# The last row of a decoder block: final product in two column halves, the norm's weight multiplied ahead of the root, the last scaling split over three store queues

## The chip, the cores and the metric

The kernel runs on one core of one Trainium2 chip. A core has a matrix engine (TensorE; PE in the profile, with its weight loads as PEld), three engines for elementwise work (VectorE, DVE; ScalarE, ACT; GpSimd, POOL), and SyncE (SP), which here only starts transfers and waits for them. Matmuls write into PSUM; the other operands lie in SBUF. Transfers can be started by SyncE, ScalarE and GpSimd, each with a queue of its own (q1, q10 and q0 in the profile), and are carried out by 16 DMA engines.

The metric is the time of one execution on the device, in microseconds.

## What is computed

One layer of a decoder block on 2048 tokens of width 1024: an adaptive norm, one wide input projection, a gated linear recurrence beside dilated window attention, a gated merge, an output projection with a gated residual, and a last RMSNorm. Only its end matters here:

```python
        merged = jax.nn.sigmoid(g_r + bg_r) * y_rnn + jax.nn.sigmoid(g_a + bg_a) * y_attn
        x = x + gate[:, None, :] * (merged @ w_o[l])
    return rms_norm(x, g_final)

def rms_norm(x, g):
    xf = x.astype(jnp.float32)
    y = xf * lax.rsqrt(jnp.mean(xf * xf, axis=-1, keepdims=True) + NORM_EPS)
    return (y * g.astype(jnp.float32)).astype(x.dtype)
```

## The kernel before

The output projection is the last stage. The 2048 rows are done in eight pairs of row blocks (`NP` = 8); a block has 128 rows, so a pair is 256 x 1024. Each pair is one level of a Strassen-like scheme with seven products of 128 x 512 (x 512) blocks instead of eight (`output_pair`, L2092). Every product is done in fp32r with the operands split into a high and a low part: `mm3` (L154) makes three matmuls for each of four slices of the inner dimension, so a product is twelve matmuls of 128 x 128 weights by 128 x 512 columns, all recorded under L152.

The products of a pair gather in the PSUM tiles X, Z, W, V and Y. VectorE and GpSimd add them to `xo`, the two blocks of x that were loaded before: `cols(p, i, j)` is column half j (512 columns) of block i of pair p. A pair's seventh product (number 6, "B22", into V) completes the right half of block 0. It is done in `last_output`; for all pairs but the last it runs inside the next pair, and the row norm follows some products later.

In the last pair nothing follows, so the order is written out by hand. `tc.manual_schedule()` keeps each engine's instructions in the order of the code. After product 5 the row block 1 is finished: `last_gain` multiplies its halves by the norm's weight `gf` on GpSimd, `square` sums squares on ScalarE (an ACTIVATE, then an ACTIVATION_READ_ACCUMULATOR that writes the sum), `mean_last` joins the two halves' sums on VectorE (L2077) and takes the root on ScalarE (L2078), and `rstd_last` (L178 to L186) makes four small operations on VectorE: a reciprocal and one correction step. `mean_first` (L2074) prepares the sum of the left half of block 0. The helper `put(j)` (L2152) scales one half of block 1 on ScalarE and stores it by SyncE's queue: `put(1)` before `last_output`, `put(0)` as its argument `between`, which runs after the root of block 0.

In `last_output` of the last pair, block 0 is finished: product 6 (L2053), the add of V to `cols(p, 0, 1)` (L2054), its square, the multiplication of `cols(p, 0, 0)` by `gf` on VectorE (L2057), the mean and the root, `put(0)`, the correction, and then the scaling with y = 1/root: ScalarE scales the left half and stores it by its own queue (L2063, L2064), and VectorE scales the right half and multiplies it by `gf` in one operation (L2065), stored by SyncE's queue (L2066). At the end of the program SyncE waits for all queues (L2227).

Of the kernel before, what the change touches and what calls it, by code (L numbers as in the profile page):

```python
# [10 lines left out]
F32 = mybir.dt.float32  # L11
F32R = mybir.dt.float32r
BF16 = mybir.dt.bfloat16
I32 = mybir.dt.int32
AF = mybir.ActivationFunctionType
ALU = mybir.AluOpType
# [4 lines left out]
P = 128  # L21
S = 2048
D = 1024
KT = D // P
NB = 4
CH = 512
H = 8
KH = KT // 2
# [62 lines left out]
def decoder_block(ctx, tc, x, c, positions, g_norm, w_mod, b_mod, w_in, b_gate, conv_w, conv_b,  # L91
                  w_a, b_a, w_x, b_x, lam, w_out_rnn, w_out_attn, w_o, g_final, cst, out):
    nc = tc.nc
    cnt = [0]

    def T(pool, shape, dt, tag, **kw):
        cnt[0] += 1
        return pool.tile(shape, dt, tag=tag, name=f"{tag}_{cnt[0]}", **kw)
# [52 lines left out]
    def mm(o, l, r, st, sp, **kw):  # L151
        nc.tensor.matmul(o, lhsT=l, rhs=r, start=st, stop=sp, **kw)  # L152

    def mm3(o, lh, ll, rh, rl, first=True, last=True, **kw):  # L154
        mm(o, lh, rh, first, False, **kw)
        mm(o, lh, rl, False, False, **kw)
        mm(o, ll, rh, False, last, **kw)
# [13 lines left out]
    def rstd_first(ss):  # L171

        nc.vector.tensor_scalar(ss[:, 0], ss[:, 0], 1.0 / D, EPS, ALU.mult, ALU.add)
        nc.scalar.activation(ss[:, 1], ss[:, 0], AF.Sqrt)

    def rstd_last(ss):
        v, y, t = (ss[:, i] for i in range(3))
        nc.vector.reciprocal(y, y)  # L178
        if y.shape[1] == 1:
            nc.vector.tensor_scalar(t, y, y, v, ALU.mult, ALU.mult)  # L180
        else:
            nc.vector.tensor_tensor(t, y, y, ALU.mult)
            nc.vector.tensor_tensor(t, t, v, ALU.mult)
        nc.vector.tensor_scalar(t, t, -0.5, 1.5, ALU.mult, ALU.add)
        if y.shape[1] == 1:
            nc.vector.tensor_scalar(y, y, t, None, ALU.mult)  # L186
        else:
            nc.vector.tensor_tensor(y, y, t, ALU.mult)
# [119 lines left out]
    first, events = {}, []  # L308
# [213 lines left out]
    B = {}  # L522
# [18 lines left out]
    outv = out[0].rearrange("(n j r) d -> n r j d", n=NB, r=4)  # L541
# [167 lines left out]
    with tc.manual_schedule():  # L709
# [87 lines left out]
        for j in range(1, 4):  # L797
            k = 2 * j
# [368 lines left out]
    for t in range(6):  # L1167
        pieces = []
        i0 = t * P
        while i0 < (t + 1) * P:  # L1170
            hd, i = divmod(i0, 96)
            n = min(96 - i, (t + 1) * P - i0)
# [156 lines left out]
    for f in range(2):  # L1329
# [20 lines left out]
        n = 0  # L1350
# [527 lines left out]
    with tc.manual_schedule():  # L1878
# [6 lines left out]
        first = min(s for s, _ in plan)  # L1885
# [48 lines left out]
    v = {}  # L1934
    tt = nc.vector.tensor_tensor
# [34 lines left out]
    A, ops = {}, {}  # L1970
    NP = 2 * NB
# [41 lines left out]
    XO, SS = {}, {}  # L2013
# [7 lines left out]
    def cols(p, i, j):  # L2021
        return XO[p, i][:, j * CH : (j + 1) * CH]

    def square(p, i, js=(0, 2)):
        if (p, i) not in SS:
            SS[p, i] = T(up[0], [P, 3, 1], F32, "ss", bufs=4)
        jk = T(up[0], [P, D], BF16, "jk", bufs=1)
        c = slice(js[0] * CH, js[1] * CH)
        nc.scalar.activation(jk[:, c], XO[p, i][:, c], AF.Square, accum_out=SS[p, i][:, 2 if js == (0, 1) else 0])
# [8 lines left out]
    up, n_p, psum = [], [0], {}  # L2038

    def product(p, i, ps, b, first, last):  # L2040
        bh, bl = B[b]
        s = ops.pop(7 * p + i)
        for k in range(KH):
            mm3(ps[:], s[:, 0, k, :], s[:, 1, k, :], bh[:, k, :], bl[:, k, :],
                first=first and k == 0, last=last and k == KH - 1, skip_group_check=True)
        n_p[0] += 1
# [3 lines left out]

    def last_output(p, between=None):
        u2, V = psum.pop(p)
        product(p, 6, V, "B22", False, True)  # L2053
        tt(cols(p, 0, 1), V[:], cols(p, 0, 1), ALU.add)  # L2054
        if p == NP - 1:
            square(p, 0, (1, 2))
            tt(cols(p, 0, 0), cols(p, 0, 0), v["gf"][:, :CH], ALU.mult)  # L2057
            mean_last(SS[p, 0], 0, 2)
            between()
            n, r = divmod(2 * p, 4)  # L2060
            rstd_last(SS[p, 0])
            y = SS.pop((p, 0))[:, 1]
            nc.scalar.activation(cols(p, 0, 0), cols(p, 0, 0), AF.Copy, scale=y)  # L2063
            nc.scalar.dma_start(outv[n, r, :, :CH], cols(p, 0, 0))  # L2064
            nc.vector.scalar_tensor_tensor(cols(p, 0, 1), cols(p, 0, 1), y, v["gf"][:, CH:], ALU.mult, ALU.mult)  # L2065
            nc.sync.dma_start(outv[n, r, :, CH:], cols(p, 0, 1))  # L2066
            return
        n = n_p[0]
        on_p(n + 1, square, p, 0)
        on_p(n + 2, lambda: rstd_first(SS[p, 0]))  # L2070
        on_p(n + 3, finish_row, p, 0)

    def mean_first(ss, i):
        nc.vector.tensor_scalar(ss[:, i], ss[:, i], 1.0 / D, EPS, ALU.mult, ALU.add)  # L2074

    def mean_last(ss, i, j):
        nc.vector.scalar_tensor_tensor(ss[:, 0], ss[:, i], 1.0 / D, ss[:, j], ALU.mult, ALU.add)  # L2077
        nc.scalar.activation(ss[:, 1], ss[:, 0], AF.Sqrt)  # L2078
# [6 lines left out]
    def on_p(n, fn, *args):  # L2085
        after.setdefault(n, []).append((fn, args))
# [5 lines left out]
    def output_pair(p):  # L2092
# [6 lines left out]
        if p:  # L2099
            last_output(p - 1)  # L2100
            fire_p()
# [35 lines left out]
        if p == NP - 1:  # L2137
            fire_p()
            square(p, 1, (0, 1))
            last_gain(p, 0)  # L2140
            mean_first(SS[p, 1], 0)
            row_start()
            fire_p()
            mean_last(SS[p, 1], 2, 0)
            square(p, 0, (0, 1))
            rstd_last(SS[p, 1])
            mean_first(SS[p, 0], 2)
            n, r = divmod(2 * p, 4)
            y = SS.pop((p, 1))[:, 1]

            def put(j):
                nc.scalar.activation(cols(p, 1, j), cols(p, 1, j), AF.Copy, scale=y)  # L2152
                nc.sync.dma_start(outv[n, r + 1, :, j * CH : (j + 1) * CH], cols(p, 1, j))

            put(1)
            last_output(p, lambda: put(0))
            return
# [74 lines left out]
```

## Time and profile before

| | us |
|---|---|
| median of 3 runs (lowest, highest) | 2160.59 (2159.23, 2162.57) |
| the profiled execution's own time | 2161.23 |
| its span, first to last instruction | 2159.4 |
| first matmul of the last product | 2148.75 |
| last scaling begins | 2154.58 |
| last stores issued (ScalarE, SyncE) | 2155.33, 2155.36 |

The granted clock of TensorE was 0.998 of full speed on average. In the profile a line of the timeline has the start and the duration in us, the engine, the line of the code, the operation, output and inputs by the program's names, shapes, and how many instructions are merged; in brackets stands how long the engine was idle before it and what ended that. A line of the groups has the number of instructions, then busy us and mean ns. Durations of instructions that follow each other overlap a little, so a group is best timed from start to start.

### The profile page before, as it was taken

To read this page: it belongs to the slowest core of one execution; us is meant where nothing else is said; L and a number is where in the kernel's file an instruction comes from. 1 tells how busy PE (TensorE), PEld (TensorE's weight loads), DVE (VectorE), ACT (ScalarE), POOL (GpSimd) and SP (SyncE) were. 2 spreads that over 40 slices of the span, in tenths; PEclk is the share of its full clock that TensorE was granted. 3 is DMA by queue.
4 is the path that set the end of the run, shared out by engine and by line. 5 is a ranking of instruction groups with operands and counts; after the bars stand their busy time and mean duration, and the time that the engine had idled before them with its cause. 6 is when DMAs were issued, how large, how long until landed. Compare 5 with 4: busy or idle time off the path is not lost.

```text
span 2159.4 us, 32571 instructions
## 1 busy us (share of the span) xinstructions
PE 2136.6 (99%) x10539; PEld 1788.3 (83%) x10539; DVE 1463.3 (68%) x2582; ACT 1296.2 (60%) x2592; POOL 1120.6 (52%) x868
## 2 busy tenths in 40 slices
PE   9999999999999999999999999999999999999998
PEld 6888778888888888888888887889898988878887
DVE  6759878768656715544436684587777687788777
ACT  5748668668644527457457532677788888443333
POOL 1467667777666423223223675466666664432555
PEclk9999999999999999999999999999999999999999
DMA  8467887887655368899997676888887777899543
GB/s 301 142 211 256 280 290 264 288 294 244 174 115 166 108 229 291 301 305 311 323 318 240 152 173 171 300 269 263 273 275 218 256 236 239 300 316 300 181 170 114
DMA packets 416575, 521.39 MB, mean 241 GB/s; under 512 B 107574, under 2 KB 282898, under 8 KB 415380
## 3 DMA queue, kind: packets, MB, share of 16 engines
q1 hardware_dynamic: 376388, 401.65, 59.7%
q10 hardware_dynamic: 34384, 99.78, 12.2%
q0 software_dynamic: 5632, 17.88, 2.6%
q8 instruction: 83, 1.36, 0.3%
q14 instruction: 88, 0.72, 0.1%
HBM read 332.02 MB, written 187.17 MB: 240 GB/s over the span
## 4 chain that ended last, share of the span: by engine, by line
PE 71%; DVE 4%; DMA 3%; issue 1%; POOL 1%; ACT 1%; SPq 0%; ACTq 0%; POOLq 0%; DVEq 0%
PE X L152 14%; PE V L152 13%; PE pj L152 12%; PE Z L152 7%; PE W L152 7%; PE Y L152 6%; PE sc L152 4%; PE o L152 4%; PE pg L152 1%; PE pT L1568 1%; PE pT L1581 1%; DMA fg<-gaT 1%; DMA kraw<-kqT 1%; DVE ptl L169 1%; DVE yl L169 1%
## 5 line engine op out<-in xcount | busy, mean ns | idle before, releaser
L166 POOL TENSOR_TENSOR S<-R,S 128x512 fp32r<-128x512 f32 x192 | 295.3, 1546 | 169.3 <-ACT S L160 82.9
L152 PE MATMUL V<-T,S 128*128 128x512 f32 x1344 | 324.3, 390 | 1.9 <-DVE ev L461 1.9
L152 PE MATMUL X<-T,S 128*128 128x512 f32 x1344 | 323.8, 390 | 1.6 <-ACT u L391 1.3
L152 PE MATMUL pj<-yh,S 128*128 128x512 f32 x896 | 321.6, 402 | 1.3 <-DVE fg L1795 0.8
L152 PEld LDWEIGHTS X<-T,S 128*128 128x128 f32 x1344 | 251.8, 188 | 56.5 <-ACT u L391 2.9
L152 PEld LDWEIGHTS V<-T,S 128*128 128x128 f32 x1344 | 251.9, 188 | 55.9 <-issue 1.9
L166 POOL TENSOR_TENSOR S<-s,S 128x512 fp32r<-128x512 f32 x116 | 173.3, 1494 | 150.1 <-ACT S L160 114.3
L152 PEld LDWEIGHTS pj<-yh,S 128*128 128x128 f32 x896 | 168.3, 188 | 32.3 <-DVE S L169 1.3
L1481 ACT ACTIVATE pp<-pp,st 128x256 f32<-128x256 f32 (+3 forms) x256 | 133.8, 524 | 78.0 <-DVE st L1480 77.4
L152 PE MATMUL pj<-yl,S 128*128 128x512 f32 x448 | 175.5, 392 | 1.0 <-POOL yl L166 1.0
L160 ACT ACTIVATE S<-s 128x512 fp32r<-128x512 f32 x124 | 77.3, 624 | 145.1 <-DVE s L291 92.1
L152 PE MATMUL W<-T,S 128*128 128x512 f32 x672 | 161.6, 389 | 0.0
L152 PE MATMUL Y<-T,S 128*128 128x512 f32 x672 | 161.6, 389 | 0.0
L152 PE MATMUL Z<-T,S 128*128 128x512 f32 x672 | 161.4, 389 | 0.0
L160 ACT ACTIVATE S<-R 128x512 fp32r<-128x512 f32 x200 | 121.5, 622 | 59.0 <-DMA R<-in_w_in_dram 14.8
L169 DVE TENSOR_TENSOR ptl<-pT,pth 128x384 fp32r<-128x384 f32 (+1 forms) x160 | 97.8, 628 | 80.5 <-ACT pth L160 78.4
L152 PEld LDWEIGHTS W<-T,S 128*128 128x128 f32 x672 | 126.0, 188 | 26.9 <-issue 0.9
L152 PEld LDWEIGHTS Z<-T,S 128*128 128x128 f32 x672 | 126.2, 188 | 26.2
L152 PEld LDWEIGHTS Y<-T,S 128*128 128x128 f32 x672 | 126.1, 188 | 26.1
L166 POOL TENSOR_TENSOR s<-R,s 128x512 fp32r<-128x512 f32 x32 | 43.2, 1350 | 188.8 <-ACT s L160 164.6
L980 DVE SCALAR_TENSOR_TENSOR xc<-xr,par,xc 128x512 f32<-128x512 f32 x96 | 102.0, 1062 | 52.1 <-ACT xc L974 49.9
L1548 ACT ACTIVATE pp<-pp,M 128x256 f32<-128x256 f32 (+3 forms) x256 | 118.0, 523 | 12.8 <-DVE M L1680 12.8
(419 smaller groups left out, 4906.0 us busy)
## 6 DMA issues: line engine op xcount, KB each, us to landing
sD<-S ACTq DMA_DIRECT2D x140, 512.0 KB, 3.7
S<-sD SPq DMA_DIRECT2D x140, 512.0 KB, 5.0
S<-wD SPq DMA_DIRECT2D x82, 512.0 KB, 5.5
R<-in_w_in_dram SPq DMA_DIRECT2D x144, 256.0 KB, 3.3
wD<-s ACTq DMA_DIRECT2D x64, 256.0 KB, 5.1
kraw<-kqT SPq DMA_DIRECT2D x32, 384.0 KB, 5.1
T<-in_w_mod_dram SPq DMA_DIRECT2D x16, 512.0 KB, 9.1
vN<-ev SPq DMA_DIRECT2D x32, 256.0 KB, 2.7
```

Of the source, the lines that this page charges most:

```text
L152: nc.tensor.matmul(o, lhsT=l, rhs=r, start=st, stop=sp, **kw)
L160: nc.scalar.activation(o, i, AF.Copy)
L166: nc.gpsimd.tensor_tensor(o, i, h.bitcast(F32), ALU.subtract)
L169: return nc.vector.tensor_tensor(o, i, h.bitcast(F32), ALU.subtract).ins
L980: nc.vector.scalar_tensor_tensor(xc, xr[:, i : i + CH], cw(i), xc, ALU.mult, ALU.add)
L1481: nc.scalar.activation(pdst, pdst, AF.Exp, bias=m_, scale=-1.0, accum_out=l_)
L1548: nc.scalar.activation(pp, pp, AF.Copy, scale=w)
L1568: nc.tensor.transpose(pt[:, c0 + j * P : c0 + (j + 1) * P], pp[i][:, k * P : (k + 1) * P], ident)
L1581: nc.tensor.transpose(pt[:, c * P : (c + 1) * P], pp[:, half * P : (half + 1) * P], ident)
```

## The change

`last_output` hands the last pair over to a new function, `last_row`, at once. It differs from the old branch in these points.

- Product 6 is done in two column halves of 256: twelve matmuls for the left 256 columns of V, then twelve for the right. After each half come its add into `xb`, its square, its product with `gf` (into a tile `g` with the tag "u1") and its part of the mean.
- `cols(p, 0, 0)` is multiplied by `gf` on GpSimd, not on VectorE.
- The weight `gf` of the right half is multiplied in ahead of the root, so the last scaling is by y alone.
- The last scaling is split: ScalarE takes the left 384 columns (stored by its queue), VectorE the right 512 (SyncE's queue) and then columns 384 to 512 (GpSimd's queue).

The root, `put(0)` (as `between`) and the correction step stay in the same order.

```diff
     def last_output(p, between=None):
         u2, V = psum.pop(p)
+        if p == NP - 1:
+            last_row(p, V, between)
+            return
         product(p, 6, V, "B22", False, True)
         tt(cols(p, 0, 1), V[:], cols(p, 0, 1), ALU.add)
-        if p == NP - 1:
-            square(p, 0, (1, 2))
-            tt(cols(p, 0, 0), cols(p, 0, 0), v["gf"][:, :CH], ALU.mult)
-            mean_last(SS[p, 0], 0, 2)
-            between()
-            n, r = divmod(2 * p, 4)
-            rstd_last(SS[p, 0])
-            y = SS.pop((p, 0))[:, 1]
-            nc.scalar.activation(cols(p, 0, 0), cols(p, 0, 0), AF.Copy, scale=y)
-            nc.scalar.dma_start(outv[n, r, :, :CH], cols(p, 0, 0))
-            nc.vector.scalar_tensor_tensor(cols(p, 0, 1), cols(p, 0, 1), y, v["gf"][:, CH:], ALU.mult, ALU.mult)
-            nc.sync.dma_start(outv[n, r, :, CH:], cols(p, 0, 1))
-            return
...
+    def last_row(p, V, between):
+        (bh, bl), s_, ss = B["B22"], ops.pop(7 * p + 6), SS[p, 0]
+        xa, xb = cols(p, 0, 0), cols(p, 0, 1)
+        jk = T(up[0], [P, D], BF16, "jk", bufs=1)
+        g = T(up[0], [P, CH], F32, "u1")
+        nc.gpsimd.tensor_tensor(xa, xa, v["gf"][:, :CH], ALU.mult)
+        for c in range(2):
+            h = slice(c * 2 * P, (c + 1) * 2 * P)
+            for k in range(KH):
+                mm3(V[:, h], s_[:, 0, k, :], s_[:, 1, k, :], bh[:, k, h], bl[:, k, h], first=False, last=k == KH - 1,
+                    skip_group_check=True)
+            tt(xb[:, h], V[:, h], xb[:, h], ALU.add)
+            nc.scalar.activation(jk[:, h], xb[:, h], AF.Square, accum_out=ss[:, 0])
+            tt(g[:, h], xb[:, h], v["gf"][:, CH + c * 2 * P : CH + (c + 1) * 2 * P], ALU.mult)
+            o = 0 if c else 2
+            nc.vector.scalar_tensor_tensor(ss[:, o], ss[:, 0], 1.0 / D, ss[:, 2], ALU.mult, ALU.add)
+        m, y, t = (ss[:, i] for i in range(3))
+        nc.scalar.activation(y, m, AF.Sqrt)
+        between()
+        nc.vector.reciprocal(y, y)
+        nc.vector.tensor_scalar(t, y, y, m, ALU.mult, ALU.mult)
+        nc.vector.tensor_scalar(t, t, -0.5, 1.5, ALU.mult, ALU.add)
+        nc.vector.tensor_scalar(y, y, t, None, ALU.mult)
+        n, r = divmod(2 * p, 4)
+        cut = 3 * P
+        nc.scalar.activation(xa[:, :cut], xa[:, :cut], AF.Copy, scale=y)
+        nc.scalar.dma_start(outv[n, r, :, :cut], xa[:, :cut])
+        nc.vector.tensor_scalar(g[:], g[:], y, None, ALU.mult)
+        nc.sync.dma_start(outv[n, r, :, CH:], g[:])
+        nc.vector.tensor_scalar(xa[:, cut:], xa[:, cut:], y, None, ALU.mult)
+        nc.gpsimd.dma_start(outv[n, r, :, cut:CH], xa[:, cut:])
```

## The prediction

> **What bounds the kernel now.** The page says that TensorE is busy for 2136.6 of 2159.4 us. The change leaves all of that alone except the last 2.9 us, and touches what comes behind them. So I read the chain of waits from 2148 us on.
>
> ```profile
> PE 2136.6 (99%) x10539; PEld 1788.3 (83%) x10539; DVE 1463.3 (68%) x2582; ACT 1296.2 (60%) x2592; POOL 1120.6 (52%) x868
> ```
>
> ```profile
> 2148.91 2.73 PE V L152 x12
> ...
> 2151.67 0.70 DVE xo L2054
> ...
> 2152.45 0.73 ACT jk L2029 x2
> ...
> 2153.20 0.17 DVE ss L2077
> ...
> 2154.58 0.75 DVE xo L2065
> ```
>
> The chain is the twelve matmuls of product 6, the add (L2054), the square, the mean (L2077), the root with its correction (2153.20 to 2154.58, 1.38 us from the mean to the last scaling), and L2065. The timeline of the same stretch shows what each engine does meanwhile.
>
> ```profile
> 2148.75 0.39 PE L152 MATMUL V<-B22h,S 128*128 128x512 f32 x1
> ...
> 2149.55 0.37 DVE L2077 SCALAR_TENSOR_TENSOR ss<-ss 128x1 f32<-128x1 f32 x1
> ...
> 2150.59 0.19 ACT L2029 ACTIVATION_READ_ACCUMULATOR jk<-xo 128x1 f32 x1
> ...
> 2151.02 0.14 DVE L2074 TENSOR_SCALAR ss<-ss 128x1 f32<-128x1 f32 x1
> 2151.19 0.72 ACT L2152 ACTIVATE xo<-xo,ss 128x512 f32<-128x512 f32 x1 [0.41 <-issue]
> 2151.24 0.39 PE L152 MATMUL V<-B22h,S 128*128 128x512 f32 x1
> 2151.67 0.69 DVE L2054 TENSOR_TENSOR xo<-V,xo 128x512 f32<-128x512 f32 x1 [0.50 <-PE V L152]
> ...
> 2152.27 0.68 DVE L2057 TENSOR_TENSOR xo<-xo,gf 128x512 f32<-128x512 f32 x1
> 2152.45 0.63 ACT L2029 ACTIVATE jk<-xo 128x512 bf16<-128x512 f32 x1 [0.54 <-DVE xo L2054]
> ...
> 2154.58 0.72 ACT L2063 ACTIVATE xo<-xo,ss 128x512 f32<-128x512 f32 x1 [0.36 <-DVE ss L186]
> 2155.33 0.37 ACTq L2064 DMA_DIRECT2D out_dram<-xo  x1
> 2155.36 0.33 SPq L2066 DMA_DIRECT2D out_dram<-xo  x1
> ```
>
> And of SyncE's list of waits (who waited for whom: us in all, times, longest):
>
> ```profile
> SPq L2227 <- DMA out_dram<-xo: 2.3, 1, 2.3
> ```
>
> After its last issue, at about 2155.8, SyncE waits 2.3 us for the stores, so it sees the last one landed at about 2158.1, 2.77 us after ScalarE issued its store. From there to the end of the span are 1.3 us. Between the span (2159.4) and the profiled run's own time (2161.23) lie another 1.8 us. The whole tail behind TensorE is thus some 8 us, 0.36% of the time.
>
> **The change part by part.**
>
> *The product in halves.* Twelve matmuls of 512 columns become 24 of 256, each with its weights loaded anew. The attention's scores show matmuls of this shape.
>
> ```profile
> 1365.03 1.60 PE L152 MATMUL sc<-kq,q 128*128 128x256 f32 x12
> ...
> 1365.95 0.42 DVE L1480 CUSTOM_DVE_ANT_0 pp<-sc,msk 128x256 f32<-128x256 f32 x1 [2.23 <-PE sc L152]
> ...
> 1366.47 0.39 PE L152 MATMUL pj<-yh,S 128*128 128x512 f32 x1
> ```
>
> Twelve take (1366.47 - 1365.03) / 12 = 0.12 us each from start to start, and one lasts 1.60 - 11 x 0.12 = 0.28 us. The left half of V is therefore complete at 2148.75 + 11 x 0.12 + 0.28 = 2150.35 us. Run without a pause, the right half would end at 2148.75 + 23 x 0.12 + 0.28 = 2151.79, against 2151.24 + 0.39 = 2151.63 now: 0.16 us of cost for the narrower form.
>
> *The pause between the halves.* V is one tile of 128x512 f32. The score rows show how such a tile is guarded. Each tile of sc holds two 128x256 parts, three matmuls each. The left part is done at 1365.03 + 2 x 0.12 + 0.28 = 1365.55, but VectorE, idle for 2.23 us, reads it only at 1365.95, when the sixth matmul, the last into the right part, has ended (1365.03 + 5 x 0.12 + 0.28 = 1365.91). The order is kept for the whole tile, not for its columns. I take it to hold in the other direction also: the right half's matmuls, which write V, wait until VectorE has read the left half. The trace of before has no matmul into a tile that is being read, so this is a choice; the other value is rival A. The Trainium skill, PSUM — Partial Sum Buffer, section PSUM bank collisions raise a hardware error, speaks against this change: two engines may not touch one bank in the same quadrant at once, disjoint columns included. By that rule a wait must stand here; by columns alone the time would be that of rival A.
>
> VectorE is late for that read. The root of row 1 keeps it until L2074, so the left add starts at about 2151.1 and, as the 256-wide row above with one operand in PSUM and one in SBUF, takes 0.42: 2151.52. A matmul that waited for VectorE's read of V shows the restart:
>
> ```profile
> 297.85 0.69 DVE L461 TENSOR_TENSOR ev<-V,u 128x512 f32<-128x512 f32 x1 [1.41 <-PE W L152]
> ...
> 298.69 0.70 PE L152 MATMUL V<-T,S 128*128 128x512 f32 x2 [1.46 <-DVE ev L461]
> ...
> 1633.61 0.30 PE L1568 MATMUL pT<-cs,pp 128*128 128x128 f32 x1 [2.09 <-ACT pp L1548]
> ```
>
> The table by stretches has the granted clock as the third number from the end:
>
> ```profile
> 296.00:300.00 4.00, 2.54 (x12) 1.81 (x11) 2.56 (x4) 1.65 (x3) 1.28 (x1) 1.00 0.81 274
> ...
> 1636.00:1638.00 2.00, 2.00 (x12) 2.00 (x10) 0.62 (x4) 2.00 (x9) 2.00 (x4) 0.50 0.16 48
> ```
>
> VectorE ended at 298.54, TensorE started 0.15 later, and this gap of 1.46 us left the granted clock at 1.00 (one of 2.09 us was followed by 0.50). So the right half starts at 2151.67 after a gap of about 1.3 us, and ends at 2151.67 + 11 x 0.12 + 0.28 = 2153.27. Nothing else is queued behind these matmuls. With an immediate restart it would be 0.15 less; a halved clock would double the 0.12, 1.3 us more. I take neither.
>
> *Add, square, mean.* The right add: 2153.31 to 2153.73. The square starts 0.09 later, as now (2151.67 + 0.69 to 2152.45). Its width halves:
>
> ```profile
> L160 ACT ACTIVATE vh<-vraw 128x256 fp32r<-128x256 f32 x32 | 12.9, 404 | 0.0
> ...
> L1548 ACT ACTIVATE pp<-pp,M 128x384 f32<-128x384 f32 x32 | 19.5, 609 | 5.5 <-DVE M L1680 5.5
> ...
> L674 DVE TENSOR_SCALAR acc<-T,ca 128x512 f32<-128x512 f32 x4 | 1.9, 483 | 1.1 <-DMA T<-in_w_mod_dram 1.0
> ...
> L1063 DVE TENSOR_SCALAR an<-an 128x128 f32<-128x128 f32 x2 | 0.4, 218 | 0.0
> ```
>
> With 0.40 instead of 0.63 the mean follows 0.75 - 0.22 = 0.53 us after the square's start: 2153.82 + 0.53 = 2154.35, **1.15 later** than now. The left half's square and mean lie in the 1.6 us of the right half's matmuls. The left mean makes VectorE wait for the left square, which stands behind the first `put` on ScalarE (2151.19 + 0.72); queued behind it are the right add and gain, needed only from 2153.3, so it is free here; in rival A it is not.
>
> *The gains.* L2057 moves from VectorE to GpSimd. It can start when ScalarE's square has read its operand: 2150.59 + 0.19 + 0.09 = 2150.87, and ends at 2152.16 by the 1.29 below, long before 2155. The left gain, with both operands in SBUF, stands against it:
>
> ```profile
> 2140.28 1.28 DVE L2035 SCALAR_TENSOR_TENSOR xo<-xo,ss,gf 128x1024 f32<-128x1024 f32 x1
> ...
> 2145.11 2.01 DVE L2035 SCALAR_TENSOR_TENSOR xo<-xo,ss,gf 128x1024 f32<-128x1024 f32 x1
> ...
> 2146.00 2.27 POOL L2081 TENSOR_TENSOR xo<-xo,gf 128x512 f32<-128x512 f32 x1
> ...
> 2148.62 1.29 POOL L2081 TENSOR_TENSOR xo<-xo,gf 128x512 f32<-128x512 f32 x1 [0.35 <-ACT jk L2029]
> ```
>
> Beside GpSimd such an operation stretches from 1.28 to 2.01, and the mean of row 1 (0.37 against 0.17 for that of block 0) ended with GpSimd's at 2149.92. The left gain would wait until 2152.2 and end near 2152.4: again inside the pause. The right gain (2153.64 to 2154.1) lies beside the right square.
>
> *Root and scaling.* The same instructions; the second `put`, still behind the root, is done before the result: y comes at 2154.58 + 1.15 = 2155.73. Then in parallel:
> - ScalarE scales 384 columns: 0.61, issue at 2156.37 (now 2155.33).
> - VectorE scales the 512 columns by a scalar alone: 0.48 instead of 0.75, SyncE's issue at 2156.24 (now 2155.36).
> - VectorE then scales 128 columns: 2156.12 to 2156.34, and GpSimd issues at 2156.4.
>
> At the present 2.77 us ScalarE's store is seen at 2156.37 + 2.77 = 2159.14.
>
> *The third queue.* No store by GpSimd's queue stands alone in the trace. The nearest:
>
> ```profile
> meT<-R POOLq DMA_DIRECT2D x2, 256.0 KB, 3.0
> ...
> meT<-R POOLq DMA_DIRECT2D x24, 256.0 KB, 5.3
> ...
> meT<-R POOLq DMA_DIRECT2D x1, 256.0 KB, 8.0
> ...
> DMA to landing us min/median/max: 2.0/2.6/3.0
> ```
>
> Four answers: 3.0 us from issue to landing between 1991 and 1999 us, where hardly another queue moved data; the median of all; the one of 2001.85 us, beside saturated loads; and, for all stores to the output by the other queues, 2.0 to 3.0. Ends: 2.0 and 8.0. I take 3.0, the quiet row; here 64 KB go instead of 256, but beside two other stores. Landing: 2156.4 + 3.0 = **2159.4**, the last of the three. The Trainium skill, DMA: Bandwidth & Descriptors, section Anatomy of one DMA — SWDGE (gpsimd) path, fits 2.0 us plus the bytes over 436 GB/s, an estimate of 2.15 us here; then ScalarE's store would be last and the sum 1.0 instead of 1.3.
>
> **Sum**: 2159.4 against 2158.1, so +1.3 us: +1.15 (pause and narrower matmuls, less the narrower add and square), -0.10 (ScalarE's 384 columns), +0.25 (GpSimd's store behind it). The span becomes 2160.7 and the profiled run 2162.5; on the median of the runs, 2160.59, that is **2161.9 us**. A measurement of this kernel can tell about 0.2%, 4.3 us, from no change.
>
> **The rivals.**
>
> *A, no pause* (order kept by columns). For it: nothing in the trace shows a matmul held in this way; against it, the 1365.95 row. TensorE ends at 2151.79, but VectorE runs left add, left gain, left mean, right add in this order: left gain until 2152.4, left mean behind it at about 2152.45 (the left square, 2151.8 to 2152.35, is no earlier), right add 2152.55 to 2152.97, mean at 2153.59: +0.39. GpSimd's store is issued at 2155.64 and lands at 2158.64, +0.5 us: 2161.1.
>
> *B, the halves overlap as written*, neither pause nor left mean and gain in the way: right add 2151.83 to 2152.25, mean 2152.87, 0.33 earlier than now; ScalarE's store 0.43 earlier, seen at 2157.67, GpSimd's at 2154.92 + 3.0 = 2157.92: -0.2 us, 2160.4. Against it: ScalarE's `put` until 2151.91 stands ahead of the left square.
>
> *C, slower*: GpSimd's store takes the end. With the 8.0 us of the third row it lands at 2164.4, +6.3 us: 2166.9. It counts as slower from a landing of 6.0 us on (2158.1 + 4.3 - 2156.4). For it: the median of 24 is 5.3; against it: those ran beside full queues, here half a megabyte is in flight.
>
> **How the numbers follow.** Forecast 0.62, A 0.23, B 0.08, C 0.04, others 0.03. All but C lie within 4.3 us: same 0.95, slower 0.04 (C), faster 0.01, since even B gains 0.2. The low end is A less the 1.4 us by which the lowest run lies under the median, 2159.7. The high end is the forecast with 5.3 instead of 3.0 us for GpSimd's store, 2161.9 + 2.3 = 2164.2.
>
> **What would show it.** The pause: a gap of 1.2 to 1.4 us in TensorE after the twelfth matmul of 256 columns, ended by the left add; without it A or B. The left mean before the right add in VectorE's order, by 0.5 us or more. The mean at about 2154.35. GpSimd's issue near 2156.4 and SyncE's last wait ended by its store about 3 us later. The prediction is wrong if TensorE runs through, if the root's chain gets shorter than 1.38 us, or if that store lands before ScalarE's.

## The result: 0.2% slower, and the profile after

| us | before | after |
|---|---|---|
| median of the runs taken together (lowest, highest), 10 each | 2160.48 (2158.81, 2162.57) | 2165.24 (2163.7, 2169.9) |
| the profiled execution's own time | 2161.23 | 2166.06 |
| its span | 2159.4 | 2164.3 |
| first matmul of the last product | 2148.75 | 2148.77 |
| from there to the end of the span | 10.7 | 15.5 |

The ratio is 1.0022, 95% interval 1.0014 to 1.0030. The forecast was 2161.9 and its range ended at 2164.2. The two profiled executions reach the last product within 0.02 us of each other, so all of the 4.9 us lie in the tail. First the timeline of the changed kernel there (start, duration, engine, line):

```profile
2150.88 1.28 POOL L2068 TENSOR_TENSOR xo<-xo,gf 128x512 f32<-128x512 f32 x1 [0.94 <-DVE ss L184]
...
2151.11 0.42 DVE L2074 TENSOR_TENSOR xo<-V,xo 128x256 f32<-128x256 f32 x1
...
2151.55 0.88 DVE L2076 TENSOR_TENSOR u<-xo,gf 128x256 f32<-128x256 f32 x1
2151.57 0.39 PE L152 MATMUL V<-B22h,S 128*128 128x256 f32 x1 [1.22 <-DVE xo L2074]
...
2152.99 0.28 PE L152 MATMUL V<-B22h,S 128*128 128x256 f32 x1
2153.30 0.42 DVE L2074 TENSOR_TENSOR xo<-V,xo 128x256 f32<-128x256 f32 x1 [0.78 <-PE V L152]
...
2154.36 0.16 DVE L2078 SCALAR_TENSOR_TENSOR ss<-ss 128x1 f32<-128x1 f32 x1 [0.17 <-ACT jk L2075]
...
2155.74 0.49 DVE L2090 TENSOR_SCALAR u<-u,ss 128x512 f32<-128x512 f32 x1
...
2156.14 0.28 DVE L2092 TENSOR_SCALAR xo<-xo,ss 128x128 f32<-128x128 f32 x1
2156.25 0.33 SPq L2091 DMA_DIRECT2D out_dram<-u  x1
2156.43 0.36 ACTq L2089 DMA_DIRECT2D out_dram<-xo  x1
2156.72 0.58 POOL L2093 DMA_DIRECT2D out_dram<-xo  x1 [4.57 <-DVE xo L2092]
```

Up to here it went nearly as forecast: the pause, the mean, the last scaling. But the last store is issued at 2157.30 and the span ends 7 us later. The transfers don't fill that time. This is GpSimd's store in the view of the DMA issues (size, us from issue to landing), which puts its landing at 2156.72 + 2.3 = 2159.0:

```profile
out_dram<-xo POOLq DMA_DIRECT2D x1, 64.0 KB, 2.3
```

SyncE's list of waits says the same. At the end of the program (now L2249) it has 2.3 us of waits for stores, and then one of 4.3 us for something else, where before there was one of 0.5 us:

```profile
SPq L2249 <- PEq L2249: 4.8, 2, 4.3
SPq L2249 <- DMA out_dram<-u: 1.7, 1, 1.7
SPq L2249 <- DMA out_dram<-xo: 0.6, 2, 0.4
```

The name of the releaser is inferred here, and TensorE cannot be it: its last matmul ended at 2153.27. The view of the line L2249 itself shows who was late. All engines meet there, and each first executes a DRAIN (count, shortest, median and longest in ns, first and last start):

```profile
L2249 POOLq DRAIN  x3: 51/98/6794, 2156.7 to 2164.0; - x3
L2249 SPq DRAIN  x3: 7/7/7, 2159.4 to 2163.8; - x3
L2249 PEldq DRAIN  x2: 13/845/1677, 2151.6 to 2163.8; - x2
L2249 DVEq DRAIN  x2: 19/370/722, 2155.8 to 2163.8; - x2
L2249 ACTq DRAIN  x2: 8/80/152, 2156.8 to 2163.8; - x2
```

SyncE is there at 2159.4, VectorE, ScalarE and TensorE earlier. GpSimd's first DRAIN begins at 2156.7 with its last instruction and lasts 6.79 us, until 2163.5, **6.2 us after that instruction has ended** (2157.30). Then the end of the program runs, 0.8 us. The kernel before has these rows at its end line, and the second fence in SyncE's list of waits:

```profile
L2227 POOLq DRAIN  x3: 51/97/7454, 2148.6 to 2159.1; - x3
L2227 SPq DRAIN  x3: 7/7/7, 2158.6 to 2158.9; - x3
```

```profile
SPq L2227 <- PEq L2227: 0.7, 2, 0.5
```

The DRAIN ends at 2148.6 + 7.45 = 2156.0, 6.1 us after GpSimd's last multiply (2148.62 + 1.29 = 2149.91). There SyncE's first DRAIN came at 2158.6, so 2.6 us of cover hid GpSimd's. The change moved GpSimd's last instruction from 2149.91 to 2157.30.

### The profile page after: what moved, and what is told of

The parts are those of the page before. It is cut to its first block, busy times and chain, and to the rows that moved or that the text cites. A ratio compares the mean times of both kernels' runs of the same rounds, so it can differ in the third digit from the quotient of the medians.

```text
span 2164.3 us, 32604 instructions
## 1 busy us (share of the span) xinstructions
PE 2137.0 (99%) x10551; PEld 1787.9 (83%) x10551; DVE 1467.5 (68%) x2586; ACT 1296.1 (60%) x2594; POOL 1122.0 (52%) x870
## 4 chain that ended last, share of the span: by engine, by line
PE 69%; DVE 5%; DMA 3%; issue 2%; POOL 1%; ACT 1%; SPq 0%; ACTq 0%; POOLq 0%; DVEq 0%
PE X L152 14%; PE V L152 14%; PE pj L152 10%; PE Z L152 7%; PE W L152 7%; PE Y L152 6%; PE sc L152 4%; PE o L152 4%; DMA fg<-gaT 2%; PE pg L152 1%; PE pT L1568 1%; PE pT L1581 1%; DMA kraw<-kqT 1%; DVE ptl L169 1%; DVE yl L169 1%
```

## The experiments

Three theories stood at first. D: the end waits for GpSimd's DRAIN, whatever its last instruction is. S: a store on GpSimd's queue is what costs. P: the pause between the halves costs it. Since profiled executions reach the tail at different times, the column "tail" counts from the first matmul of the last product to the end of the span. "Drain" is from the end of GpSimd's last instruction to the end of its first DRAIN at the program's end. "SyncE ready" is the start of SyncE's first DRAIN there, when it has seen the stores. All times in us come from one profiled execution of each run.

| run | drain | drain ends | SyncE ready | span ends | tail | ratio to before (95%) |
|---|---|---|---|---|---|---|
| before | 6.12 | 2156.0 | 2158.6 | 2159.4 | 10.7 | |
| after | 6.19 | 2163.5 | 2159.4 | 2164.3 | 15.5 | 1.0022 (1.0014, 1.0030) |
| e1 third store by SyncE | 6.12 | 2157.7 | 2158.7 | 2159.6 | 11.4 | 1.0000 (0.9989, 1.0011) |
| e2 before + tiny GpSimd op | 6.12 | 2160.5 | 2157.4 | 2161.3 | 13.7 | 1.0012 (1.0002, 1.0022) |
| e3 before + GpSimd store | 6.19 | 2160.5 | 2156.7 | 2161.3 | 14.4 | 1.0021 (1.0012, 1.0030) |
| e4 e1 + PSUM tiles apart | 6.12 | 2158.5 | 2158.7 | 2159.5 | 10.5 | 1.0001 (0.9991, 1.0010) |
| e5 early GpSimd store | 6.21 | 2161.0 | 2160.9 | 2161.8 | 12.3 | 1.0004 (0.9994, 1.0013) |
| e6 e2, 0 transfers by GpSimd | 0.07 | 2163.1 | 2165.9 | 2166.6 | 10.4 | 1.0028 (1.0016, 1.0041) |
| e7 version put together | 6.13 | 2157.7 | 2158.1 | 2158.9 | 10.4 | 0.9992 (0.9983, 1.0000) |
| e8 e2, 30 transfers | 2.53 | 2157.4 | 2157.7 | 2158.5 | 10.5 | one run, 2160.32 beside 2160.17 |
| e9 e2, 6 transfers | 0.57 | 2157.1 | 2159.4 | 2160.2 | 10.5 | one run, 2162.02 beside 2160.17 |
| e10 after, 1 transfer | 1.67 | 2169.4 | 2169.5 | 2170.3 | 11.2 | one run, 2172.11 beside 2160.17 |
| e11 after, 31 transfers | 3.03 | 2160.9 | 2160.2 | 2161.7 | 12.3 | 1.0011 (1.0002, 1.0019) |
| e12 e7, 30 transfers | 2.53 | 2152.8 | 2156.5 | 2157.3 | 10.2 | 0.9994 (0.9985, 1.0003) |

### e1: the third store on another queue

```diff
-        nc.gpsimd.dma_start(outv[n, r, :, cut:CH], xa[:, cut:])
+        nc.sync.dma_start(outv[n, r, :, cut:CH], xa[:, cut:])
```

> The changed kernel with its third store (columns 384 to 512) issued by SyncE's queue instead of GpSimd's; all else as in the change. Theory D (GpSimd's drain at the end of the program lasts about 6.15 us from the end of its last instruction, whatever that is): the last instruction is now the gain, ending at 2152.15, so the drain ends near 2158.3 and hides behind the stores; the span falls from 2164.3 to 2160.0 to 2160.4, 4 us less than the change, 0.6 to 1.0 more than before. Theory S (only a software store at the end is followed by a long drain): the same here. Rival P (the pause and the narrower matmuls make the loss): the span stays near 2164.

GpSimd's last instruction and its DRAIN rows:

```profile
2150.29 1.27 POOL L2068 TENSOR_TENSOR xo<-xo,gf 128x512 f32<-128x512 f32 x1 [0.94 <-DVE ss L184]
```

```profile
L2249 POOLq DRAIN  x3: 51/98/7434, 2150.3 to 2159.3; - x3
```

The DRAIN ends at 2157.7, before SyncE has seen the stores. The loss is gone, and with it 4.1 of the 4.9 us of the tail, though the pause of 1.21 us is still there. All that is left of the change, the pause included, lengthens the tail by 0.7 us, and P falls. S and D are both alive.

### e2: a tiny GpSimd operation late in the kernel before

```diff
+            nc.gpsimd.tensor_tensor(ss[:, 2], cols(p, 0, 0)[:, :1], cols(p, 0, 0)[:, :1], ALU.mult)
```

It stands behind ScalarE's last scaling, multiplies one column and nobody reads the product.

> The kernel before, with one GpSimd multiplication of 128x1 added behind ScalarE's last scaling, whose result nobody uses. Theory D: it ends near 2155.5, the drain near 2161.7, and the span grows by about 3 us from 2159.4 to 2162.3. Theory S: no store, so the drain is hidden as before and the span stays at 2159.4 within 0.2.

The timeline, the view of the end line and SyncE's waits:

```profile
2154.17 0.19 POOL L2066 TENSOR_TENSOR ss<-xo 128x1 f32<-128x1 f32 x1 [5.47 <-ACT xo L2064]
```

```profile
L2229 POOLq DRAIN  x3: 51/98/6354, 2154.1 to 2161.0; - x3
```

```profile
SPq L2229 <- PEq L2229: 3.7, 2, 3.2
SPq L2229 <- DMA out_dram<-xo: 2.3, 1, 2.3
```

An operation of 0.19 us that moves nothing lengthens the tail by 3.1 us: GpSimd is drained at 2160.5, SyncE was ready at 2157.4. S falls as the whole story.

### e3: the kernel before with a small store by GpSimd

```diff
-            nc.scalar.dma_start(outv[n, r, :, :CH], cols(p, 0, 0))
+            nc.scalar.dma_start(outv[n, r, :, : 3 * P], cols(p, 0, 0)[:, : 3 * P])
+            nc.gpsimd.dma_start(outv[n, r, :, 3 * P : CH], cols(p, 0, 0)[:, 3 * P :])
```

> The kernel before, with the last quarter (128 columns) of the left half's store issued by GpSimd's queue, and the rest by ScalarE's as before. No halves, no pause. Theories D and S: GpSimd's store ends near 2156.0, the drain near 2162.1, the span at about 2162.9, 3.5 us more than before. Rival P: the span grows by less than 1 us.

```profile
2153.76 0.58 POOL L2065 DMA_DIRECT2D out_dram<-xo  x1 [5.68 <-ACT xo L2063]
```

```profile
L2228 POOLq DRAIN  x3: 51/98/6792, 2153.7 to 2161.0; - x3
```

This one edit, without halves, gains or a new split of the scaling, gives the ratio of the whole change (1.0021); its tail grew by 3.7 of the 4.9 us. The store had landed 2.6 us after its issue; the DRAIN went on for another 4.2 us.

### e4: the halves without the pause

```diff
+        U = [new_sum("Z"), new_sum("W")]
...
-                mm3(V[:, h], s_[:, 0, k, :], s_[:, 1, k, :], bh[:, k, h], bl[:, k, h], first=False, last=k == KH - 1,
+                mm3(U[c][:, h], s_[:, 0, k, :], s_[:, 1, k, :], bh[:, k, h], bl[:, k, h], first=k == 0, last=k == KH - 1,
...
+            tt(cols(p, 0, 1), V[:], cols(p, 0, 1), ALU.add)
```

On top of e1 the two halves gather in two other PSUM tiles, and what V holds already is added to the row block earlier.

> The changed kernel with the third store by SyncE's queue, and the two halves of the last product in two PSUM tiles of their own; product 3's part of V is added to the row ahead of them by one more VectorE operation. Order of all else as in the change. If the gap of 1.22 us in TensorE came from sharing the tile, it is gone: TensorE runs through to about 2151.8, the mean (L2078, second) comes at 2153.6 instead of 2154.36, and the span is 0.6 to 0.8 below that of e1_third_on_sync. If the gap stays (a wait on VectorE for another reason), so does the mean at 2154.3 and the span equals e1's.

Timeline:

```profile
2150.28 0.28 PE L152 MATMUL Z<-B22h,S 128*128 128x256 f32 x1
...
2150.40 0.28 PE L152 MATMUL W<-B22h,S 128*128 128x256 f32 x1
...
2151.76 0.89 DVE L2077 TENSOR_TENSOR u<-xo,gf 128x256 f32<-128x256 f32 x1
...
2152.64 0.42 DVE L2075 TENSOR_TENSOR xo<-W,xo 128x256 f32<-128x256 f32 x1
...
2153.70 0.16 DVE L2079 SCALAR_TENSOR_TENSOR ss<-ss 128x1 f32<-128x1 f32 x1 [0.18 <-ACT jk L2076]
```

TensorE goes from the left half to the right without a gap. So the pause came from reading one half of a PSUM tile while the other was to be written. The Trainium skill, PSUM — Partial Sum Buffer, section PSUM bank collisions raise a hardware error, gives the reason why such a wait must stand; the gap of 1.22 us, gone with tiles of their own, agrees, though no run here tells whether the bank or the tile decides. The right add still waits for VectorE's left gain until 2152.64, where the matmuls ended at 2152.00. The tail is 0.9 us shorter than in e1, 0.15 shorter than before.

### e5: a GpSimd store that isn't last

```diff
-                nc.sync.dma_start(outv[n, r + 1, :, j * CH : (j + 1) * CH], cols(p, 1, j))
+                (nc.gpsimd if j else nc.sync).dma_start(outv[n, r + 1, :, j * CH : (j + 1) * CH], cols(p, 1, j))
```

> Third store on SyncE's queue as in e1, and the right half of row 1 (128x512, issued some 3 us after the first matmul of the last product) stored from GpSimd's queue instead of SyncE's. GpSimd works in order, so its multiply by the norm's weight comes behind that store: its last operation ends about 5.0 us after the first matmul (3.2 + 0.6 for the issue + 1.29). Theory D (the end waits for GpSimd's own drain, about 6.13 us behind its last instruction, whatever that was): the drain ends at 5.0 + 6.13 = 11.1 and the span at about 12.0 us after the first matmul, some 0.6 later than e1's 11.4; ratio to before 1.0003. Rival S (a store on the software queue in the tail costs some 4 us by itself, wherever it stands): the span ends 15 to 16 us after the first matmul, ratio 1.002.

```profile
2152.94 0.58 POOL L2175 DMA_DIRECT2D out_dram<-xo  x1 [2.30 <-ACT xo L2174]
2153.54 1.28 POOL L2068 TENSOR_TENSOR xo<-xo,gf 128x512 f32<-128x512 f32 x1
```

```profile
L2249 POOLq DRAIN  x3: 51/98/8079, 2152.9 to 2161.5; - x3
```

The drain ends 6.2 us after the multiply, at 2161.0, as D has it. The tail is 12.3 us (D 12.0, S 15 to 16), which speaks against S, but it isn't a measure of the drain alone. The multiply, now behind the store, ran beside VectorE's left mean, and this 128 x 1 operation took 1.77 us and ended with it, at 2154.85. So the right add came late, and SyncE was ready only at 2160.9, 0.2 us ahead of the drain's end and, from the first matmul, 0.8 later than in e1. The early store thus has a price of its own by what it pushes back, but not the 4 us of S.

### e6, e8, e9: what sets the length of the drain

All three are e2 with fewer transfers on GpSimd's queue; the others go to SyncE. The DMA issues of the kernel before show, beside the 24 `meT<-R`, what that queue is given: two groups of 22 loads, and six small loads into `prow` (the first and the last of them shown). That makes 74 transfers, the last one at 2002 us, 150 us before the end.

```profile
fg<-gaT POOLq DMA_DIRECT2D x22, 256.0 KB, 6.4
fg<-mrT POOLq DMA_DIRECT2D x22, 256.0 KB, 7.1
...
prow<-in_b_mod_dram POOLq DMA_DIRECT2D x1, 12.0 KB, 5.7
...
prow<-in_lam_dram POOLq DMA_DIRECT2D x1, 4.0 KB, 5.5
```

```diff
-        (nc.scalar if i in (0, 2, 4) else nc.gpsimd).dma_start(prow[r0 : r0 + ap.shape[0], :], ap)
+        (nc.scalar if i in (0, 2, 4) else nc.sync).dma_start(prow[r0 : r0 + ap.shape[0], :], ap)
...
-                (nc.gpsimd if t > TAIL0 + 1 else nc.sync).dma_start(g[:], src[at_])
+                nc.sync.dma_start(g[:], src[at_])
...
-            (nc.gpsimd if t >= TAIL0 else nc.sync).dma_start((mrT if ys is yaT else meT)[m * P : (m + 1) * P, n * CH : (n + 1) * CH], G.pop(t)[0][:])
+            nc.sync.dma_start((mrT if ys is yaT else meT)[m * P : (m + 1) * P, n * CH : (n + 1) * CH], G.pop(t)[0][:])
```

e6 has all three edits (no transfer left), e8 the second alone (30 left), e9 the second and third (6 left).

> The kernel before with the tiny GpSimd multiply of e2 behind the last scaling, and with none of its transfers on GpSimd's queue (the ten or so that it issues in earlier stages go to SyncE and ScalarE). Theory D (the drain takes its 6.1 us whatever GpSimd did before): drain 6.1 us behind the tiny multiply, SyncE waits some 3 us at the end as in e2, last matmul to end of span about 10.9 us. Rival Q (the drain empties the software queue, and is that long because the program used it): drain under 1 us behind the tiny multiply, last matmul to end of span 7.8 to 8.0 us as before. The ratio may move by the transfers of the earlier stages in either case; the drain's row tells.

The tiny operation and the DRAIN of e6:

```profile
2162.81 0.20 POOL L2066 TENSOR_TENSOR ss<-xo 128x1 f32<-128x1 f32 x1 [5.46 <-ACT xo L2064]
```

```profile
L2229 POOLq DRAIN  x3: 34/78/297, 2162.8 to 2166.4; - x3
```

The longest DRAIN is 0.30 us, 0.07 behind the operation. So "6.1 us whatever GpSimd did" was wrong, and Q was right about the cause, though not as the emptying of something still under way: in the kernel before the last transfer is 150 us old. The whole kernel lost 0.28% by the moved transfers, in earlier stages. Beside that, the drains of all runs so far had come in two sizes, 6.12 to 6.13 with 74 transfers and 6.19 to 6.21 with 75. This gave the next theory, N: a fixed time for every transfer that the queue has ever been given.

> The kernel of e2 (tiny GpSimd multiply behind the last scaling), with the 44 gate and partial-sum loads of L1789 on SyncE's queue: GpSimd's queue is left with 30 of its 74 transfers, the last of them some 150 us before the end. Theory N (the drain takes a fixed time for each transfer that GpSimd's queue was ever given: 74 of them 6.12 to 6.13 us, 75 of them 6.19 to 6.21, none 0.07, so 0.08 us each): 0.07 + 30 x 0.082 = 2.5 us. Rival F (a fixed 6.1 us, whenever the queue was used at all): 6.1 us. Rival Z (by bytes: 17.9 MB took 6.1): about 2.2 us.

```profile
2154.67 0.20 POOL L2066 TENSOR_TENSOR ss<-xo 128x1 f32<-128x1 f32 x1 [5.47 <-ACT xo L2064]
```

```profile
L2229 POOLq DRAIN  x3: 51/102/2762, 2154.6 to 2158.2; - x3
```

> As e8, with the 24 stores of L1803 on SyncE's queue too: six small transfers of the program's first microseconds (L649) are all that GpSimd's queue is given. Theory N: 0.07 + 6 x 0.082 = 0.56 us. Rival F: 6.1 us. Rival Z: about 0.1 us, as six rows of a few KB are hardly any bytes.

```profile
2156.38 0.19 POOL L2066 TENSOR_TENSOR ss<-xo 128x1 f32<-128x1 f32 x1 [5.48 <-ACT xo L2064]
```

```profile
L2229 POOLq DRAIN  x3: 45/102/796, 2156.3 to 2159.9; - x3
```

30 transfers: 2.53 us (N 2.5, F 6.1, Z 2.2). Six, of 44 KB together, in the first microseconds of the program: 0.57 (N 0.56, F 6.1, Z 0.1). The number of transfers sets it, not their bytes and not how long ago they were: (6.12 - 0.07) / 74 = **0.082 us each**.

### e10, e11: the changed kernel with fewer transfers on that queue

e10 is the changed kernel with the three edits of e6, e11 with the second alone.

> The changed kernel as it is, third store on GpSimd's queue included, with the 74 earlier transfers of that queue on SyncE's and ScalarE's. Theory N: one transfer, so the drain behind the third store's issue takes about 0.15 us, SyncE no longer waits at the end for GpSimd but for the store to be seen (2.3 us behind its issue), and the span ends about 11.4 us after the first matmul of the last product, where the changed kernel takes 15.5 and the kernel before 10.65: what the prediction had summed, 1.3 us more than before, within 0.6. Rival F: drain 6.1 us, span 15.5 us after the first matmul. The whole time is no measure here, since the moved transfers slow the earlier stages (e6 lost 0.28% with them).

```profile
2167.06 0.71 POOL L2093 DMA_DIRECT2D out_dram<-xo  x1 [4.56 <-DVE xo L2092]
```

```profile
L2249 POOLq DRAIN  x3: 40/89/2402, 2167.0 to 2170.1; - x3
```

The drain was expected to take 0.15 us and took 1.67: it ended at 2169.44, 0.08 after the store had landed (2167.06 + 2.3 = 2169.36). The one transfer was still under way, and the drain lasted until just behind its landing, by about the 0.08 us that N counts for one transfer; N had left the wait out. The end of the span is as expected, 11.2 us behind the first matmul: with the store where the change puts it, on GpSimd's queue, the change lengthens the tail by 0.6 us against the kernel before, 0.8 against e6, which has the same transfers moved.

> The changed kernel as it is, third store on GpSimd's queue included, with the 44 loads of L1789 on SyncE's queue: 31 transfers on GpSimd's. Theory N: drain 0.07 + 31 x 0.082 = 2.6 us behind the third store's issue, 3.6 less than in the changed kernel; the span ends some 12.0 us after the first matmul of the last product (15.5 in the changed kernel, 10.65 before), ratio to before 1.0005 (the changed kernel 1.0022). Rival F: 15.5 us, ratio 1.002.

```profile
L2249 POOLq DRAIN  x3: 51/102/3637, 2157.3 to 2161.4; - x3
```

The drain is half of what it was and sets the end still, 0.7 us behind SyncE; the ratio falls to 1.0011. It took 3.03 us, 0.4 more than N's 2.6. Here too the store was under way for the first 1.7 us of it. That the drain stopped at this store and then went on with the rest would fit, but no run shows the order in which it goes. In after and e3, where the store was under way just as long, the drain with 75 transfers took no more than the sum.

### e7, e12: a version put together

On top of e4, both adds stand ahead of the multiply of the right half by the weight, GpSimd multiplies 384 columns only, and the last scaling is in two pieces:

```diff
-        nc.gpsimd.tensor_tensor(xa, xa, v["gf"][:, :CH], ALU.mult)
+        nc.gpsimd.tensor_tensor(xa[:, :cut], xa[:, :cut], v["gf"][:, :cut], ALU.mult)
...
-        g = T(up[0], [P, CH], F32, "u1")
+        g = T(up[0], [P, D - cut], F32, "gg")
...
-        nc.sync.dma_start(outv[n, r, :, CH:], g[:])
+        nc.sync.dma_start(outv[n, r, :, cut:], g[:])
-        nc.vector.tensor_scalar(xa[:, cut:], xa[:, cut:], y, None, ALU.mult)
-        nc.sync.dma_start(outv[n, r, :, cut:CH], xa[:, cut:])
```

> A version put together from what the runs showed: the two halves in PSUM tiles of their own (as e4), both adds ahead of the weight's multiply on VectorE, GpSimd's multiply on 384 columns alone, last scaling in two pieces and two stores (384 columns by ScalarE, 640 by VectorE and SyncE). Theory D: GpSimd's last operation ends 3.1 us after the first matmul, its drain at 9.2, beside SyncE's last store wait; the mean comes 4.2 us after the first matmul (before 4.45, e4 4.73), the scaled row is issued 1.0 us after the root's last step (before 1.15), and the span ends 10.1 to 10.4 us after the first matmul (before 10.65, after 15.5). Ratio to before 0.9998, that is no difference that can be measured; to the changed kernel about 0.998. If the drain is not the cause, the shared PSUM tile and the third store's queue would be worth 1 us together, and the ratio to before would stay near 1.0015.

> The kernel of e7 with the same 44 loads on SyncE's queue. Theory N: GpSimd's drain ends some 3.6 us earlier than in e7, but it was hidden there by 0.4 us, so at most the end comes as in e7, 10.4 us after the first matmul; ratio 0.9992 as e7, that is nothing more is to be had at the end of this kernel from the drain.

Timeline of e7, from the first matmul of the last product on:

```profile
2148.48 0.28 PE L152 MATMUL Z<-B22h,S 128*128 128x256 f32 x1
...
2152.12 0.69 DVE L2079 TENSOR_TENSOR gg<-xo,gf 128x512 f32<-128x512 f32 x1
...
2152.99 0.16 DVE L2081 SCALAR_TENSOR_TENSOR ss<-ss 128x1 f32<-128x1 f32 x1
...
2155.06 0.36 ACTq L2093 DMA_DIRECT2D out_dram<-xo  x1
```

The mean missed its place: 4.5 us behind the first matmul instead of 4.2, as the multiply of 0.69 us and the left mean keep VectorE until then. The tail is 10.4 us, 0.25 less than before, and in e12 10.2; the drain was hidden in both, so this last difference isn't its work. The ratio of e7 to before, 0.9992, has an interval that touches 1.0, and e12's holds it, so neither is shown to beat the kernel before. Against the changed kernel the medians on their chips, each held against before, make it about 0.3% (1.0022 and 0.9992).

## Why the prediction was wrong, by its own steps

- **Product in halves, pause: right.** The gap is 1.22 us (forecast about 1.3), the right half starts at 2151.57 (2151.67) and ends at 2153.27 (2153.27). That the end is met exactly is luck: the restart came 0.1 us earlier than forecast, and the twelve matmuls took 1.70 us instead of 1.60, as the second started 0.23 behind the first. The granted clock was 1.00 in this stretch, as taken. e4 shows the cause that rival A denied. Rival A's price for an unbroken product, +0.39 us on the mean, was near: e4's mean comes 4.73 us after the first matmul, before 4.45, +0.28, held up by the left gain as A said.
- **Add, square, mean: right.** Mean at 2154.36 (2154.35). The square of 256 columns takes 0.42 (0.40).
- **Gains: right.** GpSimd's from 2150.88 to 2152.16 (2150.87 to 2152.16); VectorE's left gain stretched to 0.88 us beside it and ended at 2152.43 (2152.4).
- **Root and scaling: right.** Last scaling at 2155.74 (2155.73), issues at 2156.25 and 2156.43 (2156.24 and 2156.37); GpSimd's at 2156.72 (2156.4), as the scaling of its 128 columns ended 0.08 later than forecast (2156.14 + 0.28 = 2156.42) and GpSimd began the issue 0.30 behind that, not 0.06.
- **The third queue: the step that failed.** Its landing was over-priced, 2.3 us instead of 3.0; the Trainium skill, DMA: Bandwidth & Descriptors, section Anatomy of one DMA — SWDGE (gpsimd) path, whose fit gave the estimate of 2.15, was closer. But the landing was the wrong thing to price. "From there to the end of the span are 1.3 us" took the last store for the last event of the program, and the prediction let the span end that much behind it. What ends last is GpSimd's DRAIN, whose 6.1 to 6.2 us count from the end of GpSimd's last instruction; the prediction has no term for it. e10, in which the DRAIN is short, shows what the rest was worth: 11.24 - 10.67 = +0.6 us instead of +1.3, 0.35 less by the earlier landing (2159.05 for 2159.4) and 0.3 less behind it, where the end follows the landing by 1.0 us and not 1.3. The remaining 15.5 - 11.2 = 4.3 us are the DRAIN.
- **Rival C** named the right instruction and the right direction (slower, through GpSimd's store) but by another mechanism: it needed a landing 6.0 us after the issue. The landing was early, and the loss came all the same. It had a chance of 0.04.

The clue was in the profile of before: the row of GpSimd's DRAIN at the end line, 7454 ns, the longest of any engine, 1.3 us of the multiply included. SyncE's wait of 0.5 us at that line was no clue: in e6, where the drain ended 2.8 us before SyncE was ready, it is 0.4. The drain's end, 2156.0, left 2.6 us of cover, and the change moved GpSimd's last instruction by 7.4 us: 7.4 - 2.6 = 4.8 us, which is what was measured. The prediction looked at what a queue transports and never asked what the engine owes at the end.

## What to carry to other kernels

At the end of a program list for each engine when its last instruction ends and how long its DRAIN is; the latest of these and of the store landings sets the end, and a queue can still cost time there, though its last transfer is 150 us old (6.1 us in the kernel before, hidden). If GpSimd has issued many transfers, let it have no instruction in the last microseconds, not even a tiny one, or give some of its transfers to other queues, and look at what those stages lose by it (with 44 moved loads e12 stands at 0.9994 beside e7's 0.9992, no loss that can be told; 74 moved transfers cost 0.28% in e6). When an edit is costed at nothing because other work hides it, write down how many microseconds of cover there are, and for which event.

## What the runs showed of the hardware that was not expected

- GpSimd's DRAIN at the end of the program took 0.07 us plus 0.082 us for each transfer that its queue was given since the start: 0, 6, 30, 74 and 75 transfers gave 0.07, 0.57, 2.53, 6.12 to 6.13 and 6.19 to 6.21 us. Neither size (4 to 256 KB) nor age mattered. It counts from the end of the engine's last instruction, be that a multiply of 128 x 1 or a store. What is done in these 0.082 us, the runs don't show.
- In e10, with one transfer, still under way, the drain ended 0.08 us behind its landing. With 31 transfers and one under way the drain took 3.03 us, 0.4 more than the sum; this is open.
- A store of 64 KB by GpSimd's queue landed 2.3 us (after) and 2.6 us (e3) after its issue, about as late as ScalarE's 192 KB, at 2.3.
